# Grouped 3x3 convolution on one core: weight masks built ahead of the loads, and whole-image rows for loads and stores

## The chip, the core and the metric

The kernel runs on one core of one Trainium2 chip. The metric is the device time of one execution in microseconds (us). The core has TensorE (PE) for matmuls, VectorE (DVE), ScalarE (ACT) and GpSimd (POOL) for other work, SyncE (SP), which here only issues DMAs, and 16 DMA engines that carry every transfer. A row of a transfer is what goes to or from one of the 128 partitions of the on-chip memory; with 128 rows on 16 engines each engine has eight rows of every transfer.

## The reference

The input `x` is 16 images of 64 channels of 64x64 float32, the weight is 128 x 8 x 3 x 3. Channels are in 8 groups: 8 input channels of a group feed 16 output channels of the same group. The output is 16 x 128 x 64 x 64 float32, 33.5 MB; the input is 16.8 MB.

```python
for g in range(groups):
    for b in range(batch):
        for co in range(c_out_per_group):
            for ci in range(c_in_per_group):
                for kh in range(k):
                    for kw in range(k):
                        output[b, g * c_out_per_group + co] += \
                            weight[g * c_out_per_group + co, ci, kh, kw] * \
                            x_pad[b, g * c_in_per_group + ci, kh:kh+h, kw:kw+w]
```

## The kernel before

**Loads.** The whole input is kept on chip as bf16, in eight tiles of 128 partitions by 64x64: `xn[0..3]` holds two images each (channels on partitions), and `xs[0..3]` holds the second eight images shifted by 32 channels, so that 32-channel quarters of four images can be fed to TensorE together. The DMA converts float32 to bf16, and all loads are issued by POOL in `load` (L53). For the first group of images there are nine loads in three cuts of the image's rows (0 to 16, 16 to 32, 32 to 64), then two halves each for the other tiles: 21 loads in all. A half-image row is 8 KB of float32 in memory and 4 KB of bf16 on chip. POOL issues eight loads at once; from the ninth on, each waits until the load eight places ahead of it has landed.

**Weights.** One small load on SP's queue brings the weight. A block mask and an identity are made from memsets on DVE (L74, L84) and three `affine_select` on POOL (L75, L79, L85), which stand in the program behind the 21 loads. DVE multiplies weight and mask into `E` (L94, five instructions), TensorE transposes `E` by the identity (L107, 18 matmuls), DVE and ACT copy the results to `wN` and `wS` (L115, L117).

**Convolution.** Four groups of images, `i` = 0 to 3, four images each. A group has eight chunks of eight image rows (`c`), a chunk has nine taps by eight streams: 72 small matmuls (32 x 64 of the array each, up to 512 columns, L131), 576 in a group and 2304 in all, each with a weight load of its own. They accumulate in four PSUM banks, one per image; there are eight banks. ACT and DVE copy the four banks (L161, L163) into output tiles `ob` of 128 x 2048 float32, half an image; there are 16 such buffers. After chunks 3 and 7 of a group SP issues four stores (L168), one per image, of 1 MB each: 128 rows of 8 KB. So output leaves in eight bursts of four stores, 32 stores in all.

The program is unrolled: nothing loops on the chip, and each engine's instructions are one long list. Instructions of one engine run in program order. The order on POOL is that of the program text, which is why the masks come behind the loads there.

Of the kernel before, what the change touches and what calls it, by code (L numbers as in the profile page):

```python
# [7 lines left out]
FP32 = mybir.dt.float32  # L8
BF16 = mybir.dt.bfloat16
ALU = mybir.AluOpType  # L10


@with_exitstack
def kernel(
    ctx: ExitStack,
    tc: tile.TileContext,
    x: bass.AP,
    weight: bass.AP,
    groups: int,
    out: bass.AP,  # L20
):
    nc = tc.nc

    B, C, H, W = x.shape
    CO, CIg, K, _ = weight.shape
    G = groups
    COg = CO // G
    HW = H * W
    T = K * K
    assert (B, C, CO, K, G, H, W) == (16, 64, 128, 3, 8, 64, 64)  # L30

    R = 8
    NCH = H // R
    HALF = HW // 2

    wpool = ctx.enter_context(tc.tile_pool(name="wpool", bufs=1))
    xpool = ctx.enter_context(tc.tile_pool(name="xpool", bufs=1))
    opool = ctx.enter_context(tc.tile_pool(name="opool", bufs=16))
    psum = ctx.enter_context(tc.tile_pool(name="psum", bufs=8, space=bass.MemoryType.PSUM))

    xr = x.rearrange("b c h w -> (b c) (h w)")
    xn = [xpool.tile([128, H, W], BF16, name=f"xn{i}") for i in range(4)]
    xs = [xpool.tile([128, H, W], BF16, name=f"xs{i}") for i in range(4)]

    def flat(t):
        return t.rearrange("p h w -> p (h w)")  # L50

    def load(t, row0, p0, p1, h0, h1):
        nc.gpsimd.dma_start(  # L53
            flat(t)[p0:p1, h0 * W : h1 * W],
            xr[row0 + p0 : row0 + p1, h0 * W : h1 * W],
        )

    w_sb = wpool.tile([128, CIg * T], FP32)
    nc.sync.dma_start(w_sb, weight.rearrange("co ci kh kw -> co (ci kh kw)"))

    cuts = [0, 16, 32, 64]
    for h0, h1 in zip(cuts, cuts[1:]):
        load(xn[0], 0, 0, 128, h0, h1)
        load(xs[3], 512 - 96, 96, 128, h0, h1)
        load(xs[0], 544, 0, 128, h0, h1)
    for i in range(1, 4):
        for h0, h1 in ((0, 32), (32, 64)):
            load(xn[i], 128 * i, 0, 128, h0, h1)
            load(xs[i], 544 + 128 * i, 0, 128 if i < 3 else 96, h0, h1)

    mask = wpool.tile([128, G], FP32)
    nc.vector.memset(mask, 1.0)  # L74
    nc.gpsimd.affine_select(  # L75
        out=mask, in_=mask, compare_op=ALU.is_ge, fill=0.0,
        base=0, channel_multiplier=1, pattern=[[-COg, G]],
    )
    nc.gpsimd.affine_select(  # L79
        out=mask, in_=mask, compare_op=ALU.is_ge, fill=0.0,  # L80
        base=COg - 1, channel_multiplier=-1, pattern=[[COg, G]],
    )
    ident = wpool.tile([128, 128], BF16)
    nc.vector.memset(ident, 0.0)  # L84
    nc.gpsimd.affine_select(  # L85
        out=ident, in_=ident, compare_op=ALU.not_equal, fill=1.0,
        base=0, channel_multiplier=1, pattern=[[-1, 128]],
    )
    E = wpool.tile([128, T, 160], BF16)
    wv = w_sb.rearrange("co (ci t) -> co t ci", t=T)  # L90
    ge = 160 // CIg
    for r in range(5):
        g0 = 4 * (r % 2)
        nc.vector.tensor_mul(  # L94
            E[:, :, 32 * r : 32 * r + 32].rearrange("p t (g c) -> p t g c", c=CIg),
            wv.unsqueeze(2).to_broadcast([128, T, 4, CIg]),
            mask[:, g0 : g0 + 4].unsqueeze(1).unsqueeze(3).to_broadcast([128, T, 4, CIg]),
        )

    wN = wpool.tile([128, T, 128], BF16)  # L100
    wS = wpool.tile([128, T, 128], BF16)
    for k, (wt, off) in enumerate(((wN, 0), (wS, 32))):
        for t0 in range(0, T, 4):
            n = min(4, T - t0)
            ps = psum.tile([128, 512], FP32, name="ps", tag="ps")
            for t in range(n):
                nc.tensor.matmul(  # L107
                    ps[:, 128 * t : 128 * t + 128],
                    E[:, t0 + t, off : off + 128],
                    ident,  # L110
                    start=True, stop=True,
                )
            dst = wt[:, t0 : t0 + n, :].rearrange("p t c -> p (t c)")
            if k == 0:
                nc.vector.tensor_copy(dst, ps[:, 0 : 128 * n])  # L115
            else:
                nc.scalar.copy(dst, ps[:, 0 : 128 * n])  # L117


    outf = out.rearrange("b co h w -> b co (h w)")  # L120
    taps = [(1, 1)] + [(a, b) for a in range(3) for b in range(3) if (a, b) != (1, 1)]

    def mm(dst, wt, xt, q, half, c, kh, kw, first, last):

        lo, hi = max(0, R * c + kh - 1), min(H, R * c + R + kh - 1)
        o0 = lo - (R * c + kh - 1)
        w0, w1 = max(0, kw - 1), min(W, W + kw - 1)
        v0 = w0 - (kw - 1)
        nr, nw = hi - lo, w1 - w0
        d3 = dst.rearrange("p (h w) -> p h w", w=W)  # L130
        nc.tensor.matmul(  # L131
            d3[64 * half : 64 * half + 64, o0 : o0 + nr, v0 : v0 + nw],
            wt[32 * q : 32 * q + 32, 3 * kh + kw, 64 * half : 64 * half + 64],
            xt[32 * q : 32 * q + 32, lo:hi, w0:w1],
            start=first, stop=last,
            tile_position=(32 * q, 64 * half),
        )

    nev = 0
    for i in range(4):  # L140
        imgs = [2 * i, 2 * i + 1, 8 + 2 * i, 9 + 2 * i]
        prev = xs[i - 1]

        streams = [
            (0, wN, xn[i], 0, 0), (2, wS, xs[i], 0, 1),
            (0, wN, xn[i], 1, 1), (3, wS, xs[i], 1, 0),
            (1, wN, xn[i], 2, 0), (3, wS, xs[i], 2, 1),
            (1, wN, xn[i], 3, 1), (2, wS, prev, 3, 0),
        ]
        obs = None  # L150
        for c in range(NCH):
            if c % 4 == 0:
                obs = [opool.tile([128, HALF], FP32, name=f"ob{i}_{c}_{b}", tag="ob") for b in range(4)]
            pcs = [psum.tile([128, 512], FP32, name="ps", tag="ps") for b in range(4)]
            for k, (kh, kw) in enumerate(taps):
                for b, wt, xt, q, half in streams:
                    mm(pcs[b], wt, xt, q, half, c, kh, kw, k == 0, k == T - 1)
            for b in range(4):
                dst = obs[b][:, 512 * (c % 4) : 512 * (c % 4) + 512]
                if nev % 2 == 0:  # L160
                    nc.scalar.copy(dst, pcs[b])  # L161
                else:
                    nc.vector.tensor_copy(dst, pcs[b])  # L163
                nev += 1
            if c % 4 == 3:
                s0 = HALF * (c // 4)
                for b in range(4):
                    nc.sync.dma_start(outf[imgs[b]][:, s0 : s0 + HALF], obs[b])  # L168


# [33 lines left out]
```

## Time and profile before

| what | value |
|---|---|
| median of three runs | 147.95 us (146.76 to 151.19) |
| the profiled execution's own time | 146.28 us |
| its span, first to last instruction | 144.5 us |
| TensorE matmuls busy | 77.0 us, 2322 instructions |
| mean granted TensorE clock | 0.908 |
| moved by DMA, as the queues count it | 42.29 MB |
| read from and written to memory | 16.81 MB and 33.55 MB |

The profile is of one execution. The span is 1.78 us shorter than that execution's time. In the page's second part the span is cut into 40 slices of 3.61 us. The GB/s row counts bytes as they arrive, and a load arrives as bf16: 213 GB/s of arriving load are 426 GB/s read from memory. In the chain of waits, "issue" is time in which an engine waited for nothing that the profile shows. Some matmul records are missing from the trace, so that a count of matmuls in a row can be a little low.

### The profile page before, as it was taken

To read this page: it belongs to the slowest core of one execution; us is meant where nothing else is said; L and a number is where in the kernel's file an instruction comes from. 1 tells how busy PE (TensorE), PEld (TensorE's weight loads), DVE (VectorE), ACT (ScalarE), POOL (GpSimd) and SP (SyncE) were. 2 spreads that over 40 slices of the span, in tenths; PEclk is the share of its full clock that TensorE was granted. 3 is DMA by queue.
4 is the path that set the end of the run, shared out by engine and by line. 5 is a ranking of instruction groups with operands and counts; after the bars stand their busy time and mean duration, and the time that the engine had idled before them with its cause. 6 is when DMAs were issued, how large, how long until landed. Compare 5 with 4: busy or idle time off the path is not lost.

```text
span 144.5 us, 4928 instructions
## 1 busy us (share of the span) xinstructions
PE 77.0 (53%) x2322; PEld 51.5 (36%) x2322; DVE 45.7 (32%) x74; ACT 37.1 (26%) x68; POOL 12.0 (8%) x28
## 2 busy tenths in 40 slices
PE   0000000049966954769792993899549499930000
PEld 0000000045733632646571672566336367620000
DVE  0000000191534526117373333355603336613000
ACT  3000000003533524214352232254503325502000
POOL 6733312300000000000000000000000000000000
PEclk9999999999999999779999699599986869999655
DMA  3999999999997996995199799749999925998991
GB/s 41 118 185 214 215 215 210 213 214 217 215 206 219 426 426 277 413 410 245 75 428 413 290 426 413 295 168 401 426 426 422 415 91 211 404 426 367 428 424 75
DMA packets 7444, 42.29 MB, mean 293 GB/s; under 512 B 992, under 2 KB 992, under 8 KB 3328
## 3 DMA queue, kind: packets, MB, share of 16 engines
q1 hardware_dynamic: 4752, 33.59, 56.0%
q0 software_dynamic: 2672, 8.39, 30.4%
q8 instruction: 18, 0.29, 0.8%
q14 instruction: 2, 0.02, 0.0%
HBM read 16.81 MB, written 33.55 MB: 348 GB/s over the span
## 4 chain that ended last, share of the span: by engine, by line
PE 53%; issue 17%; DMA 16%; DVE 2%; POOL 2%; DVEq 0%; POOLq 0%
PE ps L131 52%; DMA xs<-in_x_dram 11%; DMA xn<-in_x_dram 5%; DVE E L94 2%; PE ps L107 1%; POOL xn L53 1%; POOL xs L53 1%; DVE ob L163 0%; DVEq L199 0%; POOL ident L85 0%; POOL mask L75 0%; POOLq L199 0%; POOLq L75 0%; POOLq L185 0%
## 5 line engine op out<-in xcount | busy, mean ns | idle before, releaser
L131 PE MATMUL ps<-xs,wS 32*64 32x504 bf16 (+3 forms) x1152 | 73.7, 412 | 22.6 <-issue 22.4
L131 PE MATMUL ps<-xn,wN 32*64 32x504 bf16 (+3 forms) x1152 | 74.9, 413 | 0.0
L163 DVE COPY ob<-ps 128x512 f32<-128x512 f32 x64 | 41.2, 686 | 57.5 <-PE ps L131 57.5
L131 PEld LDWEIGHTS <-wS 32*64 32x64 bf16 x1152 | 47.3, 115 | 18.6 <-issue 3.1
L161 ACT COPY ob<-ps 128x512 f32<-128x512 f32 x64 | 34.6, 589 | 63.1 <-PE ps L131 54.3
L131 PEld LDWEIGHTS <-wN 32*64 32x64 bf16 x1152 | 40.3, 115 | 29.1 <-issue 27.8
L107 PE MATMUL ps<-ident,E 128*128 128x128 bf16 x18 | 2.1, 313 | 30.8 <-DVE E L94 30.8
L107 PEld LDWEIGHTS <-E 128*128 128x128 bf16 x18 | 1.8, 147 | 30.8 <-DVE E L94 30.8
L94 DVE TENSOR_TENSOR E<-w_sb,mask 128x288 bf16<-128x288 f32 x5 | 2.9, 643 | 27.4 <-POOL mask L79 27.4
L117 ACT CAST wS<-ps 128x512 bf16<-128x512 f32 (+1 forms) x3 | 1.2, 487 | 30.3 <-PE ps L107 30.3
L53 POOL DMA_DIRECT2D xs<-in_x_dram x12 | 6.4, 536 | 9.9 <-DMA xs<-in_x_dram 7.3
L53 POOL DMA_DIRECT2D xn<-in_x_dram x9 | 5.0, 550 | 6.0 <-DMA xn<-in_x_dram 4.6
L115 DVE CAST wN<-ps 128x512 bf16<-128x512 f32 (+1 forms) x3 | 1.5, 551 | 0.1
L117 ACT ACT_TABLE_LOAD x1 | 1.3, 1283 | 0.8 <-PEq L185 0.8
L74 DVE MEMSET mask<- 128x8 f32 x1 | 0.1, 65 | 0.9 <-PEq L185 0.9
L85 POOL TENSOR_SCALAR_AFFINE_SELECT ident<-ident 128x128 bf16<-128x128 bf16 x1 | 0.3, 298 | 0.0
L75 POOL TENSOR_SCALAR_AFFINE_SELECT mask<-mask 128x8 f32<-128x8 f32 x1 | 0.2, 204 | 0.1
L79 POOL TENSOR_SCALAR_AFFINE_SELECT mask<-mask 128x8 f32<-128x8 f32 x1 | 0.2, 191 | 0.0
L185 POOL MEMSET const-float32-0.0<- 128x1 f32 x1 | 0.1, 99 | 0.3 <-issue 0.3
L84 DVE MEMSET ident<- 128x64 uint32 x1 | 0.1, 112 | 0.0
L185 POOL MEMSET const-bfloat16-1.0<- 128x1 bf16 x1 | 0.1, 102 | 0.0
L185 POOL MEMSET const-uint8-127<- 128x1 uint8 x1 | 0.1, 102 | 0.0
(1 smaller groups left out, 0.1 us busy)
## 6 DMA issues: line engine op xcount, KB each, us to landing
out_dram<-ob SPq DMA_DIRECT2D x32, 1024.0 KB, 8.8
xn<-in_x_dram POOLq DMA_DIRECT2D x7, 512.0 KB, 17.6
xs<-in_x_dram POOLq DMA_DIRECT2D x5, 512.0 KB, 16.2
xs<-in_x_dram POOLq DMA_DIRECT2D x2, 384.0 KB, 19.4
xn<-in_x_dram POOLq DMA_DIRECT2D x2, 256.0 KB, 5.8
xs<-in_x_dram POOLq DMA_DIRECT2D x2, 256.0 KB, 6.9
xs<-in_x_dram POOLq DMA_DIRECT2D x2, 64.0 KB, 5.7
xs<-in_x_dram POOLq DMA_DIRECT2D x1, 128.0 KB, 9.5
```

What stands on the lines that cost most here:

```text
L53: nc.gpsimd.dma_start(flat(t)[p0:p1, h0 * W : h1 * W], xr[row0 + p0 : row0 + p1, h0 * W : h1 * W],)
L75: nc.gpsimd.affine_select(out=mask, in_=mask, compare_op=ALU.is_ge, fill=0.0, base=0, channel_multiplier=1, pattern=[[-COg, G]],)
L79: nc.gpsimd.affine_select(out=mask, in_=mask, compare_op=ALU.is_ge, fill=0.0, base=COg - 1, channel_multiplier=-1, pattern=[[COg, G]],)
L85: nc.gpsimd.affine_select(out=ident, in_=ident, compare_op=ALU.not_equal, fill=1.0, base=0, channel_multiplier=1, pattern=[[-1, 128]],)
L94: nc.vector.tensor_mul(E[:, :, 32 * r : 32 * r + 32].rearrange("p t (g c) -> p t g c", c=CIg), wv.unsqueeze(2).to_broadcast([128, T, 4, CIg]),
L107: nc.tensor.matmul(ps[:, 128 * t : 128 * t + 128], E[:, t0 + t, off : off + 128], ident, start=True, stop=True,)
L115: nc.vector.tensor_copy(dst, ps[:, 0 : 128 * n])
L117: nc.scalar.copy(dst, ps[:, 0 : 128 * n])
L131: nc.tensor.matmul(d3[64 * half : 64 * half + 64, o0 : o0 + nr, v0 : v0 + nw], wt[32 * q : 32 * q + 32, 3 * kh + kw, 64 * half : 64 * half ...
L161: nc.scalar.copy(dst, pcs[b])
L163: nc.vector.tensor_copy(dst, pcs[b])
L185: nc = _bacc.Bacc("TRN2", target_bir_lowering=False, num_devices=1)
```

## The change

- The two memsets and the three selects move ahead: the memsets to before all loads, the selects to directly behind the first load on POOL.
- The first group is loaded in two cuts (rows 0 to 32, 32 to 64), in the order `xn[0]`, `xs[0]`, `xs[3]` (32 partitions) for each; every other tile is one load of whole images, with rows of 16 KB in memory and 8 KB on chip. There are 12 loads instead of 21.
- Output tiles are whole images (128 x 4096 float32), in eight buffers instead of 16 halves; the bytes are the same. For groups 0, 1 and 2 there is one burst of four stores of 2 MB, in rows of 16 KB, behind chunk 7. The last group is still stored in two bursts of four stores of 1 MB.

```diff
-    opool = ctx.enter_context(tc.tile_pool(name="opool", bufs=16))
+    opool = ctx.enter_context(tc.tile_pool(name="opool", bufs=8))
...
-    cuts = [0, 16, 32, 64]
-    for h0, h1 in zip(cuts, cuts[1:]):
+    mask = wpool.tile([128, G], FP32)
+    ident = wpool.tile([128, 128], BF16)
+    nc.vector.memset(mask, 1.0)
+    nc.vector.memset(ident, 0.0)
+
+    def make_masks():
+        nc.gpsimd.affine_select(
+            out=mask, in_=mask, compare_op=ALU.is_ge, fill=0.0,
+            base=0, channel_multiplier=1, pattern=[[-COg, G]],
+        )
+        nc.gpsimd.affine_select(
+            out=mask, in_=mask, compare_op=ALU.is_ge, fill=0.0,
+            base=COg - 1, channel_multiplier=-1, pattern=[[COg, G]],
+        )
+        nc.gpsimd.affine_select(
+            out=ident, in_=ident, compare_op=ALU.not_equal, fill=1.0,
+            base=0, channel_multiplier=1, pattern=[[-1, 128]],
+        )
+
+    for h0, h1 in ((0, 32), (32, 64)):
         load(xn[0], 0, 0, 128, h0, h1)
+        if h0 == 0:
+            make_masks()
+        load(xs[0], 544, 0, 128, h0, h1)
         load(xs[3], 512 - 96, 96, 128, h0, h1)
-        load(xs[0], 544, 0, 128, h0, h1)
     for i in range(1, 4):
-        for h0, h1 in ((0, 32), (32, 64)):
-            load(xn[i], 128 * i, 0, 128, h0, h1)
-            load(xs[i], 544 + 128 * i, 0, 128 if i < 3 else 96, h0, h1)
...
+        load(xn[i], 128 * i, 0, 128, 0, H)
+        load(xs[i], 544 + 128 * i, 0, 128 if i < 3 else 96, 0, H)
...
-        obs = None
+        last = i == 3
+        obs = [opool.tile([128, HW], FP32, name=f"ob{i}_{b}", tag="ob") for b in range(4)]
         for c in range(NCH):
-            if c % 4 == 0:
-                obs = [opool.tile([128, HALF], FP32, name=f"ob{i}_{c}_{b}", tag="ob") for b in range(4)]
...
-                dst = obs[b][:, 512 * (c % 4) : 512 * (c % 4) + 512]
+                dst = obs[b][:, 512 * c : 512 * c + 512]
...
-            if c % 4 == 3:
-                s0 = HALF * (c // 4)
+            n = 4 if last else NCH
+            if c % n == n - 1:
+                s0, s1 = 512 * (c + 1 - n), 512 * (c + 1)
                 for b in range(4):
-                    nc.sync.dma_start(outf[imgs[b]][:, s0 : s0 + HALF], obs[b])
+                    nc.sync.dma_start(outf[imgs[b]][:, s0:s1], obs[b][:, s0:s1])
```

More of the change, by code (lines that the diff above doesn't have):

```diff
@@ L33 @@
     NCH = H // R
-    HALF = HW // 2
     wpool = ctx.enter_context(tc.tile_pool(name="wpool", bufs=1))
     xpool = ctx.enter_context(tc.tile_pool(name="xpool", bufs=1))
-    opool = ctx.enter_context(tc.tile_pool(name="opool", bufs=16))
+    opool = ctx.enter_context(tc.tile_pool(name="opool", bufs=8))
     psum = ctx.enter_context(tc.tile_pool(name="psum", bufs=8, space=bass.MemoryType.PSUM))
@@ L59 @@
     nc.sync.dma_start(w_sb, weight.rearrange("co ci kh kw -> co (ci kh kw)"))
-    cuts = [0, 16, 32, 64]
-    for h0, h1 in zip(cuts, cuts[1:]):
+    mask = wpool.tile([128, G], FP32)
[16 more added lines that the diff above has]
+    for h0, h1 in ((0, 32), (32, 64)):
         load(xn[0], 0, 0, 128, h0, h1)
+        if h0 == 0:
+            make_masks()
+        load(xs[0], 544, 0, 128, h0, h1)
         load(xs[3], 512 - 96, 96, 128, h0, h1)
-        load(xs[0], 544, 0, 128, h0, h1)
     for i in range(1, 4):
-        for h0, h1 in ((0, 32), (32, 64)):
-            load(xn[i], 128 * i, 0, 128, h0, h1)
-            load(xs[i], 544 + 128 * i, 0, 128 if i < 3 else 96, h0, h1)
[L73 to L88, printed above, removed]
+        load(xn[i], 128 * i, 0, 128, 0, H)
+        load(xs[i], 544 + 128 * i, 0, 128 if i < 3 else 96, 0, H)
     E = wpool.tile([128, T, 160], BF16)
```

## The prediction

> **What bounds the kernel now.** I read the page first: its busy times, its slices and its chain by engine.
>
> ```profile
> PE 77.0 (53%) x2322; PEld 51.5 (36%) x2322; DVE 45.7 (32%) x74; ACT 37.1 (26%) x68; POOL 12.0 (8%) x28
> ...
> DMA  3999999999997996995199799749999925998991
> GB/s 41 118 185 214 215 215 210 213 214 217 215 206 219 426 426 277 413 410 245 75 428 413 290 426 413 295 168 401 426 426 422 415 91 211 404 426 367 428 424 75
> ...
> q8 instruction: 18, 0.29, 0.8%
> ...
> HBM read 16.81 MB, written 33.55 MB: 348 GB/s over the span
> ...
> PE 53%; issue 17%; DMA 16%; DVE 2%; POOL 2%; DVEq 0%; POOLq 0%
> ```
>
> DMA is busy for most of the span, at one rate: loads arrive at about 213 GB/s (426 read), full slices of stores show 426. At 0.426 MB per us, 50.36 MB take 118 us; the rest of the 144.5 is the start, the end and slices in which DMA starves (19, 32). So two things alternate as the bound, DMA and what feeds the stores, which is PE. Hence the chain of waits, in order of time (start, duration, what):
>
> ```profile
> 32.87 7.82 PE ps L131 x142
> 40.69 1.22 issue
> 41.91 3.66 PE ps L131 x128
> 45.57 1.44 issue
> 47.01 3.66 PE ps L131 x128
> 50.67 1.71 issue
> 52.38 3.56 PE ps L131 x119
> 55.94 2.64 issue
> 58.58 5.29 PE ps L131 x128
> 63.87 1.18 issue
> 65.05 3.66 PE ps L131 x128
> 68.71 0.89 issue
> 69.60 7.12 PE ps L131 x256
> 76.72 2.80 issue
> 79.52 8.64 PE ps L131 x242
> 88.17 2.65 issue
> 90.82 8.68 PE ps L131 x233
> 99.50 0.15 issue
> 99.64 3.56 PE ps L131 x119
> 103.20 3.46 issue
> 106.66 5.29 PE ps L131 x128
> 111.96 2.00 issue
> 113.96 12.26 PE ps L131 x384
> 126.22 2.49 issue
> 128.71 1.64 PE ps L131 x49
> ```
>
> PE stops after every 128 matmuls or a multiple of it. 128 matmuls with their weight loads are 256 instructions. Queue q8 moved 0.29 MB of instructions in 18 packets, 16 KB each; PE has 4644 instructions, 18 times 258. So I read each stop as PE waiting for its next 16 KB of instructions, which travel through the same DMA engines as the data. I call 128 matmuls a block and the time from one block's start to the next the cadence. Two windows say when it stops (us, busy times, PEclk, DMA share, GB/s):
>
> ```profile
> 96.00:116.00 20.00, 14.40 (x440) 9.66 (x425) 7.97 (x13) 6.54 (x12) 0.00 (x0) 0.88 1.00 412
> 116.00:121.00 5.00, 5.00 (x160) 3.47 (x152) 2.35 (x4) 2.15 (x4) 0.00 (x0) 0.81 0.13 48
> ```
>
> With DMA at 1.00 PE works 14.4 of 20 us; with DMA at 0.13 it never stops. The cadences: DMA idle, 3.56 (7.12 for 256), or 4.0 where the granted clock dips (12.26 for three blocks is 4.09). Under loads, 47.01 - 41.91 = 5.10 and 52.38 - 47.01 = 5.37, mean 5.2. Under stores, 58.58 - 52.38 = 6.20, 6.47, 106.66 - 99.64 = 7.02 and 7.30; I take 6.6. A 1 MB store is 8 rows on each of 16 engines, 1.049 / 0.426 = 2.46 us; call that a share. Over 3.56 the fetch loses 1.54 to 1.81 under loads (0.6 to 0.7 share) and 2.64 to 3.74 under stores (1.1 to 1.5 shares, 9 to 12 rows). It seems to queue behind whole shares, not behind one row of 2.46 / 8 = 0.31 us.
>
> **Masks early.** This is what lets PE start:
>
> ```profile
> DVE E L94 <- POOL mask L79: 27.4, 1, 27.4
> ```
> ```profile
> 27.79 0.20 POOL mask L75
> ...
> 28.40 2.32 DVE E L94 x4
> ...
> 30.77 2.10 PE ps L107 x18
> ```
> ```profile
> w_sb<-in_weight_dram SPq DMA_DIRECT2D x1, 36.0 KB, 1.9
> ```
> ```profile
> 1.29 0.67 POOL L53 DMA_DIRECT2D xn<-in_x_dram  x1 [0.78 <-POOLq L185]
> ...
> 6.31 0.56 POOL L53 DMA_DIRECT2D xs<-in_x_dram  x1 [0.68 <-DMA xn<-in_x_dram]
> ```
>
> The three selects take 28.40 - 27.79 = 0.61 and end at about 1.96 + 0.61 = 2.6; the small weight load, on SP's queue, lands 1.9 after its issue, so by about 3. E to the first convolution matmul takes 32.87 - 28.40 = 4.5: weights stand at about 7.5. Later loads on POOL are issued 0.61 later, hidden by the first load's own share of 2.46; uncovered it would cost 0.61.
>
> Now the loads hold PE. The first three (`xn[0]`, `xs[0]`, the quarter `xs[3]`) are 2.36 MB, 5.5 us at 0.426. Transfers begin at about 2.9: slice 0 holds 41 x 3.61 = 0.15 MB arriving, 0.7 us of work before 3.61. In the profile the ninth load was let go at 6.31 by the first load landing, whose 0.52 MB would be through at 2.9 + 1.2 = 4.1; so 2 us for stragglers and landing. PE starts at 2.9 + 5.5 + 2.0 = 10.4, 22.5 earlier than 32.87. Were DMA the only other bound, the end would be 2.9 + 118 and a tail of 4.3 (below): 125, the floor.
>
> **Rows of 16 KB.** The rate of DMA itself is bounded by the store slices that are full: 401 to 428 around 426 or less. All at 428 would gain 0.5% of 118, 0.6 us; all at 401 would lose 6%, 7 us. Loads (8 KB read, 4 KB arriving) and stores (8 KB) run at the same 426 although their rows differ, so I take zero. What changes is the fetch. A share doubles to 4.92. If the fetch queues by rows or by shares, its excess doubles: under stores 3.56 + 2 x (2.64 to 3.74) = 8.8 to 11.0; if 3.56 hides part of the queue, up to 2 x 6.6 = 13.2. Under loads 6.6 to 7.2, at most 10.4. If it queues by bytes, nothing changes (6.6 and 5.2). I take doubling, 10 and 7.5, nearer to the lower ends, because a loss of 9 to 12 rows, on eight rows each, looks like shares.
>
> [...]
>
> **Whole-image stores.** Groups 0 to 2 store 8.39 MB behind chunk 7: bursts of 19.7 us instead of 9.85. SP waits for the last copy of a group, and only stores are queued behind it. Eight buffers mean group 2's copies wait for group 0's stores and group 3's for group 1's; in the sum below these are 9 us or more old by then, so free; were PE as fast as in the first rival, under 2 us.
>
> **The sum**, matmul number and time. Of the blocks, 16 lie between 41.91 and 128.71 and 49 matmuls behind, so 2304 - 2048 - 49 = 207 lie ahead: fetch boundaries at 207, 335, 463 and so on. The first 207 took 41.91 - 32.87 = 9.04, with one fetch under loads in it; plus 2.3 for the longer wait.
> - Group 0: 10.4 + 11.3 = 21.7 (207), 29.2 (335), 36.7 (463), and 113 matmuls at full rate, 3.1: done at 39.8. Loads are through at about 43.5, so DMA is busy until 41 + 2.5 + 19.7 = 63.2.
> - Group 1: 44.2 (591, fetch asked at 36.7), 54.2, 64.2 (847), then DMA idle at 4.0 a block: 68.2, 72.2 (1103), done 73.7. DMA has starved for 11 us.
> - Group 2: burst 74.9 to 94.6. 76.1 (1231, already fetched), 86.1, 96.1, 100.1 (1615), done 103.6. Starved 10 us.
> - Group 3: burst 104.8 to 124.5. 104.1 (1743), 108.1 (asked before the burst), 118.1 (1999); the half group's stores queue until 134.4; 128.1 (2127), 134.7 (8 KB rows, 6.6), done 136.2.
> - Tail: before, 144.5 - 130.35 = 14.2 from the last matmul (9.85 of stores, 4.3 for the last copy, landing and end). Span 150.4.
>
> The profiled execution of before is 1.78 longer than its span: 152.2 against its 146.28, or 4% slower. That execution is 1.1% below the median of 147.95; I do not add this, and forecast 152. With both cadences at the doubled-excess minimum (8.8, 6.6) the same steps give a span of 143 (145 us), with both doubled whole 158.7 (160 us): the forecast's own range is 145 to 160. The gain of 22.5 at the start is paid back as starved DMA: in each of three groups PE gets only two blocks through a 20 us burst and makes up the others afterwards.
>
> **Rivals.** *The fetch does not lengthen (0.22).* The wait goes by bytes or by a fixed part, cadences stay 5.2 and 6.6. For it: no data row of before is 16 KB, so nothing shows the growth. Against: loss in whole shares. Steps: group 0 done at 10.4 + 9.04 + 2 x 5.2 + 3.1 = 32.9, group 1 63.8, group 2 89.3; then DMA is continuous, 90.5 + 19.7 + 9.85 = 120, and the last burst and tail take 14.2: span 134.2, 136.0 us, 7% faster. It decides when store cadences stay under about 8.
>
> [...]
>
> *Half of the excess grows (0.18).* Part is fixed latency: 8.3 and 6.3. Group 0 done at 36.3, then 70.9, 97.7, 126.9; DMA frees at 98.9 + 19.7 + 9.85 = 128.5, plus 14.2: span 142.7, 144.5 us, 1.2% faster. For it: the excess under loads is only 0.6 share, so waits are not always whole ones.
>
> **Chances.** Doubling has 0.60. 2% is what a measurement of this kernel can tell. Doubling splits 0.38 slower, 0.19 within 2%, 0.03 faster (its low end); half growth 0.11 within, 0.07 faster; no growth 0.22 faster. So 0.32 faster, 0.30 same, 0.38 slower. The range 134 to 158 leaves out what of the no-growth case lies between the floor and 134 (0.1) and the worst of doubling (0.08).
>
> **What would show it.** Convolution starting at 10 to 11 us; stops by "issue" still every 128 matmuls but two to three times as long under bursts (6 us instead of 2.6 to 3.5); DMA slices near zero after each of the first two bursts, some 10 us each; last matmul near 136. Wrong if store cadences stay below 8, if DMA never starves (then near 135), or if PE stops elsewhere than at blocks of 128.

## The result, and the profile after

The changed kernel takes 137.73 us, the median of five runs (135.59 to 139.09), against 147.95 us before, the median of five (146.62 to 151.19). Each kernel has faster and slower executions, and the ratio of the faster ones alone (135.59 and 135.77 for the changed kernel) is 0.921, with a 95% interval of 0.911 to 0.931. It is 8% faster. The forecast was 152 and slower; the first rival, at 136.0, came closest. The profiled execution took 139.08 us with a span of 137.4.

Two rows of the page's second part, in 40 slices of 3.43 us: DMA busy tenths, and GB/s.

```profile
DMA  3999999999999999995599999206999999999991
GB/s 33 179 209 217 222 217 215 212 219 212 217 243 320 336 403 410 444 410 215 234 429 396 453 410 420 119 5 279 391 437 429 410 444 394 422 425 417 420 384 62
```

DMA starves twice, in slices 18 to 19 and 25 to 27. The windows that hold these gaps and the stretch behind them (us; busy times; PEclk, DMA share, GB/s):

```profile
64.50:67.50 3.00, 3.00 (x128) 2.07 (x112) 1.29 (x2) 1.07 (x2) 0.00 (x0) 1.00 0.23 93
89.00:95.00 6.00, 5.34 (x200) 3.90 (x207) 2.58 (x4) 2.17 (x5) 0.00 (x0) 1.00 0.22 86
97.00:119.00 22.00, 14.36 (x384) 9.16 (x384) 7.73 (x12) 6.41 (x12) 0.00 (x0) 0.84 1.00 420
```

So the gaps are there, behind the first two bursts as forecast, but about 3 and 6 us long, not 11 and 10. The chain of waits in order of time (start, duration, what) has the cadences; the convolution is line 133 now.

```profile
7.27 9.90 PE ps L133 x154
17.17 1.98 issue
19.15 5.35 PE ps L133 x128
24.50 0.85 issue
25.34 3.66 PE ps L133 x128
29.01 2.53 issue
31.54 3.56 PE ps L133 x119
35.10 2.91 issue
38.01 3.61 PE ps L133 x128
...
67.89 3.66 PE ps L133 x128
71.56 3.63 issue
75.19 4.94 PE ps L133 x111
80.12 2.63 issue
82.75 3.66 PE ps L133 x128
...
97.23 3.66 PE ps L133 x128
100.89 3.63 issue
104.52 5.35 PE ps L133 x128
109.87 1.95 issue
111.81 5.35 PE ps L133 x128
117.16 1.94 issue
119.10 1.64 PE ps L133 x49
```

PE still stops only at blocks of 128. Under loads the cadence is 6.2 (19.15, 25.34, 31.54) and 6.5; under the second burst 7.3 (67.89 to 75.19), 7.6 and 6.8, and three times 7.29 from 97.23 on. The first burst, which begins while loads are still running, has 6.7, 6.6 (two blocks in 13.22) and 6.2 (38.01 to 64.16). Forecast were 7.5 under loads and 10 under stores. A second profile of the same kernel (after_again below, an execution of 138.54 us) has 7.29, 7.57 and 6.75 in the second burst and 7.57, 7.29 and 7.02 from the third on. The last matmul ends at 120.7 and DMA still has a backlog by then (a DMA share of 0.98 and 413 GB/s from 120.74 to 134).

The prediction inferred that these stops are instruction fetches. The trace's records of single packets bear it out: queue q8 has one packet of 16 KB per block, and each stop of this chain ends 1.2 to 1.6 us after such a packet has ended. For the block that starts at 67.89, the packet runs from 72.74 to 73.70 and PE resumes at 75.19. The window of 72.70 to 73.75 holds it:

```profile
q8 instruction: 1, 0.02, 5.7%
```

With DMA full the packet itself takes 0.9 to 1.0 us every time. What changes is how long after the block's start it begins: 1.1 to 1.2 us where DMA starves, 3.7 to 4.0 under loads, 4.4 to 5.3 under the second and third bursts.

### The profile page after: what moved, and what is told of

Same layout as the page of the kernel before. It is cut to its first block, busy times and chain, and to the rows that moved or that the text cites. A ratio compares the mean times of both kernels' runs of the same rounds, so it can differ in the third digit from the quotient of the medians.

```text
span 137.4 us, 4892 instructions
## 1 busy us (share of the span) xinstructions
PE 82.1 (60%) x2322; PEld 52.5 (38%) x2322; DVE 45.8 (33%) x74; ACT 37.1 (27%) x68; POOL 7.2 (5%) x19
## 4 chain that ended last, share of the span: by engine, by line
PE 60%; issue 25%; DVE 2%; DMA 1%; DVEq 0%
PE ps L133 58%; DVE E L96 2%; PE ps L109 2%; DMA w_sb<-in_weight_dram 1%; DVE ob L164 0%; DVEq L201 0%; DVEq L96 0%
## 5 line engine op out<-in xcount | busy, mean ns | idle before, releaser
L133 PE MATMUL ps<-xs,wS 32*64 32x504 bf16 (+3 forms) x1152 | 77.2, 423 | 33.5 <-issue 33.5
L133 PE MATMUL ps<-xn,wN 32*64 32x504 bf16 (+3 forms) x1152 | 80.0, 425 | 0.0
L133 PEld LDWEIGHTS <-wS 32*64 32x64 bf16 x1152 | 48.4, 118 | 21.8 <-issue 10.0
L133 PEld LDWEIGHTS <-wN 32*64 32x64 bf16 x1152 | 40.9, 118 | 40.9 <-issue 39.9
L52 POOL DMA_DIRECT2D xs<-in_x_dram x7 | 3.7, 537 | 4.1 <-DMA xs<-in_x_dram 2.3
L52 POOL DMA_DIRECT2D xn<-in_x_dram x5 | 2.9, 575 | 1.9 <-DMA xn<-in_x_dram 1.1
```

Source lines behind the costliest of these rows:

```text
L52: nc.gpsimd.dma_start(flat(t)[p0:p1, h0 * W : h1 * W], xr[row0 + p0 : row0 + p1, h0 * W : h1 * W],)
L133: nc.tensor.matmul(d3[64 * half : 64 * half + 64, o0 : o0 + nr, v0 : v0 + nw], wt[32 * q : 32 * q + 32, 3 * kh + kw, 64 * half : 64 * half ...
```

## The experiments

**The parts of the change, done alone or undone.** Median times, each with the median of the kernel before, measured beside it on the same chip:

| run | masks | loads | stores | us | before |
|---|---|---|---|---|---|
| masks_only | early | as before | half images | 133.34 | 149.61 |
| half_loads | early | half images | whole images | 138.39 | 149.61 |
| half_stores | early | whole images | half images | 132.58 | 149.61 |
| quarter_stores | early | whole images | quarter images | 134.95 | 149.61 |
| fine_tail | early | whole images | half, last group quarter | 133.24 | 148.59 |
| rows_only | late | whole images | whole images | 146.73 | 148.05 |
| after_again | early | whole images | whole images | 138.65 | 148.05 |
| half_again | early | whole images | half images | 132.56 | 148.05 |

*masks_only*: the kernel before, with memsets and selects moved as in the change and nothing else.

```diff
     for h0, h1 in zip(cuts, cuts[1:]):
         load(xn[0], 0, 0, 128, h0, h1)
+        if h0 == 0:
+            make_masks()
```

> The kernel before with the masks moved early and nothing else: rows of 8 KB, half images, 21 loads and 32 stores stay. Theory A (the early masks bring the gain, and long rows cost a little through longer instruction fetches): PE starts at about 7 to 10 us, cadence 5.2 under loads and 6.6 under stores; 207 matmuls at 18.5, 16.4 further blocks at about 6.2, PE ends near 120, plus 14.2: span 132 to 136, as fast as the changed kernel or up to 3% faster. Theory B (the long rows bring part of the gain, by fewer DMAs and longer unbroken transfer): over 2% slower than the changed kernel, 140 us or more.

133.34 us (132.52 to 133.81): theory A's time. Its steps fit less well: PE waits for a load of `xs` until 19.25, 207 matmuls are reached at 22.95 and not at 18.5, and the cadences are 5.9 to 6.7 where DMA is full, under loads and stores alike. The masks alone give at least as much as the whole change does (135.59 to 139.09 in the five runs above, 137.99 to 139.50 in four more below). The four were on another chip, but the kernel with half-image stores, run on both, took 132.58 and 132.56. DMA starves only once, in slice 35 (115.2 to 118.5 us), as the last matmuls run:

```profile
DMA  2899999999999999999999999999999999949990
```

*half_loads*:

```diff
-        load(xn[i], 128 * i, 0, 128, 0, H)
-        load(xs[i], 544 + 128 * i, 0, 128 if i < 3 else 96, 0, H)
+        for h0, h1 in ((0, 32), (32, 64)):
+            load(xn[i], 128 * i, 0, 128, h0, h1)
+            load(xs[i], 544 + 128 * i, 0, 128 if i < 3 else 96, h0, h1)
```

> The changed kernel with the loads of groups 1 to 3 in half images again (8 KB read per row), stores as changed. Theory A: the load cadence falls from 6.2 to 5.2 for about 5 blocks, group 0 is done some 3 us earlier, DMA starves less; 132 to 136 us. Theory B: 137 us or more.

138.39 us, the time of the changed kernel. The number is theory B's, but its reason is not borne out: the load rows make no difference that can be measured. The cadence under loads was 6.20 with 8 KB rows too (blocks starting at 18.33, 24.53 and 30.73), so theory A's step from 6.2 to 5.2 was wrong.

*half_stores*, and the same kernel again (*half_again*) beside the changed one (*after_again*) on one chip:

```diff
-            n = 4 if last else NCH
+            n = 4
```

> The changed kernel with all groups stored as the last one is, in two bursts of four stores of 1 MB (8 KB rows), loads as changed. Theory A: the store cadence falls from 7.3 to about 6.6, the first burst starts half a group earlier, DMA starves at most 3 us in all; 130 to 135 us. Theory B: 138 us or more.

> The changed kernel once more, beside the half-image stores on the same chip: 135 to 139 us.

> Half-image stores with everything else of the change, beside the changed kernel on the same chip. If bursts of 2 MB stores and the starving between them are what the changed kernel loses: 132 to 133 us, 2% to 4% faster than it. If the earlier difference was the chip: within 2% of it.

132.58, and then 132.56 against 138.65 on one chip: 4.4% less. Their ratios to before are 0.902 (0.894 to 0.911) and 0.944 (0.935 to 0.953). Half-image stores beat both kernels; whole-image stores cost the change about 6 us on this chip (3 against its two quickest runs on record, 135.59 and 135.77). The chain of half_again, in a stretch with DMA full throughout:

```profile
68.46 3.66 PE ps L133 x128
72.13 2.26 issue
74.39 3.66 PE ps L133 x128
78.05 2.26 issue
80.31 5.35 PE ps L133 x128
85.65 0.57 issue
86.23 3.56 PE ps L133 x119
```

The cadence is 5.92 three times running, even where a granted clock of 0.68 stretches the matmuls of a block to 5.35.

*quarter_stores*, stores of 0.5 MB behind every second chunk, and *fine_tail*, this for the last group alone:

```diff
-            n = 4 if last else NCH
+            n = 2
```

```diff
-            n = 4 if last else NCH
+            n = 4 if i < 3 else 2
```

> The changed kernel with stores of two chunks each: bursts of four stores of 0.5 MB in rows of 4 KB, loads as changed. Theory A: shares of 1.23 us, the fetch waits less, store cadence 4.5 to 6, last burst 5 us shorter; 124 to 131 us. Theory B: rows of 4 KB cost rate and DMAs are many: 138 us or more.

> Half-image stores for groups 0 to 2 (bursts of four 1 MB stores) and two-chunk stores (0.5 MB, 4 KB rows) for the last group, whole-image loads, masks early. The half-image run starved DMA for some 4 us around the last group. If that is what still separates it from the DMA floor: 128 to 131 us, against 132.6 for half images. If small stores cost as much as in the all-quarter run: 132 to 134.

134.95 and 133.24: neither theory's numbers for quarters, and for the finer tail the second guess, no gain over half images. The chain of quarter_stores, rows of 4 KB, a share of 1.23 us:

```profile
79.47 3.66 PE ps L133 x128
83.13 2.26 issue
85.39 5.12 PE ps L133 x75
```

5.92 again: half the share, the same cadence. DMA did not starve, but from 64 to 100 us, where DMA was full in both, it ran at 414 GB/s and in half_again at 421.

*rows_only*: the selects behind the 12 loads again.

```diff
-        if h0 == 0:
-            make_masks()
...
         load(xs[i], 544 + 128 * i, 0, 128 if i < 3 else 96, 0, H)
+    make_masks()
```

> The changed kernel with the three selects behind all loads again: rows of 16 KB, whole-image stores, masks late. With 12 loads in place of 21 POOL reaches the selects earlier than before (it waits for the load eight places ahead, which are now larger: some 20 to 27 us). If the early masks bring the whole gain: PE starts 15 to 20 us later than in the changed kernel, DMA starves between the bursts, 146 to 153 us, no faster than before. If the rows bring part of it: 140 us or less.

146.73 us (143.31 to 149.42 in ten runs), not told apart from 148.05 (146.20 to 153.48 in thirteen). What let E go, by the waits:

```profile
DVE E L95 <- POOL mask L70: 13.0, 1, 13.0
```

With 12 loads POOL reaches the selects at 13 us, not at 20 to 27 as I expected, and PE starts 14 us earlier than before (18.5). Even so no clear gain is measured: the rows and whole-image bursts cost about what this earlier start is worth. How much of it is the bursts, this run alone does not tell.

**A stream beside PE.** To price the fetch by itself, these kernels convolve group 0's tiles four times over, keep the results on chip, and let SP store a constant tile; only the form of the stores differs. The edit of bg_16k_8rows, without the lines that leave out loads and results:

```diff
+    cst = opool.tile([128, HW], FP32, name="cst", bufs=1)
+    nc.vector.memset(cst, 0.5)
+    for b in range(B):
+        nc.sync.dma_start(outf[b], cst)
```

> The disputed cost by itself. The kernel loads group 0's tiles only and convolves them four times over (so all matmuls are there), its results stay on chip, and SP sends 33.5 MB of a constant tile to the output without waiting for anything: one steady stream of 79 us beside PE, then a quiet rest. Left out: the loads of groups 1 to 3 and the storing of results. Here the stream is 32 stores of 1 MB, eight rows of 8 KB on each engine. All theories: cadence as in the half-image runs under stores, 5.9 to 6.6, and 3.5 to 4.1 when the stream has ended.

> The same with 16 stores of 2 MB, eight rows of 16 KB on each engine, the form of the changed kernel. By bytes (a fetch waits for about as many bytes whatever the rows): 5.9 to 6.6. By what the changed kernel showed: 6.7 to 7.6. By whole shares or by rows, as predicted: 8.8 to 11.

> The same with 16 stores of 2 MB, but sixteen rows of 8 KB on each engine (two images, half an image each). If the length of the row sets the wait: as with 1 MB stores of 8 KB rows, 5.9 to 6.6. If the size of the DMA sets it: as with 2 MB stores of 16 KB rows, 6.7 to 7.6 or more. By bytes: 5.9 to 6.6.

> The same with 32 stores of 1 MB, four rows of 16 KB on each engine (64 partitions each). If the length of the row sets the wait: 6.7 to 7.6. If the size of the DMA sets it, or bytes: 5.9 to 6.6.

> Steady stream beside PE as before (loads of groups 1 to 3 and the storing of results left out): 16 stores of 2 MB in 16 KB rows, but from four different tiles and to the images in the order of the changed kernel. The single-tile stream had cadences of 5.9 to 6.7, mean 6.2; the changed kernel 7.3 under the same rows. If the source tiles or the images make the difference: 7.0 to 7.6. If not: 5.9 to 6.7.

The chain of bg_8k_16rows (2 MB stores, 8 KB rows), and then of bg_16k_8rows (2 MB stores, 16 KB rows), DMA share 1.0 in both:

```profile
43.81 3.66 PE ps L138 x128
47.47 2.26 issue
49.73 5.35 PE ps L138 x128
```

```profile
63.52 3.66 PE ps L134 x128
67.18 2.53 issue
69.71 5.02 PE ps L134 x110
```

The cadences are 5.92 with 8 KB rows in 2 MB stores and 6.19 with 16 KB rows. All blocks in full streams: 8 KB rows in 1 MB stores 5.92 to 6.20; 8 KB rows in 2 MB stores 5.9 to 6.2; 16 KB rows 5.92 to 6.74, mean 6.2, and from four tiles 5.9 to 6.2. Twice the share costs 0.0 to 0.3 us (0.8 in one block), not 2.6 to 3.7. That ends the doubling.

One stream does not fit: bg_16k_4rows, with 64 partitions to a store, was slower, 6.7 to 8.1. By its own condition that points at the length of the row, but the streams of 128 partitions with the same rows do not show it. Why it is slower stays open.

*bg_2k_8rows* (256 KB stores) shows that a full DMA alone does not make 5.92.

> Steady stream as in the 1 MB run, but 128 stores of 256 KB, eight rows of 2 KB on each engine, a share of 0.6 us. If the extra wait of about 2.4 us is a fixed number of bytes or a fixed latency of a busy DMA engine: 5.9 to 6.2 as with 8 KB rows, as long as DMA stays busy. If it is a number of rows or shares: 4.2 or less. If the issuing queue cannot keep DMA busy with such small stores, cadence falls and the DMA share shows it.

Two windows of this run (us; busy times; PEclk, DMA share, GB/s):

```profile
18.00:24.00 6.00, 3.66 (x128) 2.45 (x128) 2.58 (x4) 2.15 (x4) 0.00 (x0) 1.00 1.06 402
24.00:38.00 14.00, 11.25 (x400) 7.90 (x407) 6.45 (x10) 5.96 (x11) 0.00 (x0) 1.00 1.05 399
```

The block from 18.29 to 24.21 took 5.92, the next three 4.56, 4.27 and 4.55, with DMA full in both windows. After 40 us, with DMA no longer full (348 GB/s to 80 us, against 426 with 16 KB rows), they take 4.0 to 4.6. So the wait can be shorter with DMA full. Whether the short rows, the small stores or the number of stores that wait in the queue do it is not told apart (SP waited 97 times for an earlier store to land).

**Bursts.** Constant tiles again, but each group's stores are let go by its last copy.

```diff
+        nc.vector.tensor_copy(cs[i][:, 0:1], dst[:, 0:1])
+        for b in (2 * i, 2 * i + 1, 8 + 2 * i, 9 + 2 * i):
+            nc.sync.dma_start(outf[b], cs[i])
```

> The same 16 stores in four bursts of four, each let go by the last copy of a group, as in the changed kernel (constant tiles are stored, loads of groups 1 to 3 left out). If the burst makes the difference (a queue that is filled once and runs out, with DMA idle ahead of it): 6.7 to 7.6 inside bursts. If not: 5.9 to 6.7. In both, 3.5 to 4.1 between the bursts.

> The burst run again (constant tiles let go by the last copy of a group, loads of groups 1 to 3 and storing of results left out), each burst of the same 8.4 MB as eight stores of 1 MB in rows of 8 KB. With 16 KB rows cadences inside bursts were 6.8 to 7.3, mean 7.1. If bursts alone make it: the same 7.1. If row length matters in a burst: 5.9 to 6.6.

> The burst run with 8 KB rows once more, now with both halves of each constant tile let go by the last copy of a group (before, the stores of the second halves had nothing to wait for and ran ahead as a steady stream). Four bursts of eight 1 MB stores; loads of groups 1 to 3 and the storing of results left out. With 16 KB rows cadences inside bursts were 6.8 to 7.3. If bursts alone make it: 6.8 to 7.3. If row length matters in a burst: 5.9 to 6.6.

In bg_8k_burst the stores of the second halves ran ahead as a stream (5.9 to 6.2, and 5.9 to 6.5 in the bursts of four that were left), so it did not test what it was meant to. The chains of bg_16k_burst and of bg_8k_burst_b, where both halves wait:

```profile
63.34 3.66 PE ps L135 x128
67.01 3.63 issue
70.64 5.35 PE ps L135 x128
```

```profile
65.74 3.66 PE ps L135 x128
69.40 3.63 issue
73.03 4.87 PE ps L135 x112
```

7.30 with 16 KB rows and 7.29 with 8 KB rows; all blocks inside bursts take 6.7 to 7.3 in both. The 7.3 of the changed kernel comes with stores let go in bursts of 8.4 MB, whatever their rows. An idle DMA ahead of the burst is not enough: in bg_8k_burst a burst of four 1 MB stores on an idle DMA had a block of 5.92 (89.74 to 95.66). By the packet records a fetch begins 4.4 to 5.1 us after its block's start inside these bursts of 8.4 MB, and 3.5 to 3.9 us after it in the streams of 8 KB rows; the packet takes 0.9 to 1.0 us in both. Why it waits longer in a burst was not settled.

## Why the prediction was wrong

**Masks early: right, with a term mis-sized.** PE's first convolution matmul came at 7.27, not 10.4. Weights stood when forecast (7.5), and E then waited for the weight's load, no longer for the mask:

```profile
DVE E L96 <- DMA w_sb<-in_weight_dram: 1.8, 1, 1.8
```

The first matmuls run on the first load; the first one that reads `xs` starts at 10.00, near the 10.4 that I forecast for having the first three loads. 207 matmuls were reached at 19.15, against 21.7: from 10.00 they took 9.15, about the 9.04 of before, so the 2.3 that I added for a longer fetch did not come.

**Rows of 16 KB: the step that failed.** It read: "A share doubles to 4.92. If the fetch queues by rows or by shares, its excess doubles", and took 10 and 7.5. Under stores the changed kernel shows 6.2 to 7.6, and the streams, where only the form of the stores changes, show 5.92 for shares of 2.46 us and for 2 MB stores of short rows (4.92), and 6.2 for 16 KB rows; quarter_stores has 5.92 for a share of 1.23. The excess of before, 1.1 to 1.5 shares, looked like a count of shares, but I had one size of store only, and one size cannot show a proportion. A wait that does not grow with the store fits it as well, and that was the first rival.

**Cadence under loads: mis-read.** My 5.2 came from the two blocks after 41.91. Windows of before (us; busy times; PEclk, DMA share, GB/s):

```profile
41.91:47.01 5.10, 3.67 (x129) 2.44 (x128) 2.58 (x4) 2.15 (x4) 0.00 (x0) 1.00 0.81 218
47.01:52.38 5.37, 3.66 (x128) 2.43 (x128) 2.58 (x4) 2.15 (x4) 0.00 (x0) 1.00 1.02 423
```

In the first the loads were ending and DMA was not full; the second ran under stores alone (423 GB/s). Neither is a cadence under full loads. With DMA full of loads it is mostly 6.2 (5.9 to 6.5 in the changed kernel and half_loads), whether rows are 8 or 16 KB.

**DMA's own rate: right.** Streams of 16 KB rows moved 426 GB/s and of 8 KB rows 422; the zero I took for it stands.

**Whole-image stores: the term that was missing.** I gave them nothing but idle time. They also make bursts of 8.4 MB, in which the cadence is about 7.3 and not 5.9. My 6.6 was a mean over before's half-size bursts, 6.2 to 7.3.

**The sum holds with the measured cadences.** They come from the execution that is being explained, so this tests the steps and not the prices. The same steps with 6.2 and 7.3, from 19.15: group 0 done at 34.7; DMA busy until 63; group 1 66.3; burst 67.5 to 87.2; group 2 93; burst and half group 94.3 to 123.9; last matmul 121; the last burst and tail of 14.2 from 123.9 give 138.1. Measured: group 1 at 65.5, group 2 at 92.6, the last matmul at 120.7, the span 137.4. So blocks, boundaries, bursts and tail were right, and the sign turned mainly on one price, that of a fetch.

**The rivals.** The first had the mechanism (no growth with the row) and nearly the time. Its span of 134.2 is 3.2 short of the profiled 137.4, since its cadences (5.2 and 6.6) were both too low; it left out the bursts. That 137.73 lies within my range of 134 to 158 is due to this rival, which the range took in, and not to the step that I forecast from. The half-growth rival (144.5) has no support: there is next to no growth to halve.

**Stops where DMA starves and where it is full.** In the changed kernel PE stopped for 0.22 us at 67.67, where DMA starves (a share of 0.23 from 64.50 to 67.50), and for 2.5 to 3.6 us where DMA is full (shares of 1.01 to 1.06 in these stops), behind blocks that ran at the full clock (1.00).

## What to carry to other kernels

This unrolled PE program fetched its instructions by DMA while its data moved (18 packets of 16 KB on queue q8), and PE stopped at its blocks of 128 matmuls. In another kernel look whether PE stops at equal counts of matmuls, and price the stop with DMA starving, full and in bursts (here 0.22 us at 67.67 of the changed kernel, 2.26 in half_again and 3.63 in bg_16k_burst). When a wait is to be scaled to a new size, first ask whether the profile has it at two sizes; one size shows a duration, not a law. Where DMA and its producer share the bound, send output early and often enough that DMA never starves (here half-image stores took 132.56 us against 138.65); a larger transfer brought nothing here, since the rate was full already (426 against 422 GB/s).

## What the runs showed that I had not expected

- With DMA full, a block of 128 matmuls took 5.92 us in run after run, with store rows of 4 or 8 KB and stores of 0.5, 1 or 2 MB; the cadences differ by steps of about 0.27 (5.92, 6.20, 6.47, 6.74, 7.02, 7.29).
- The packet of a fetch takes 0.9 to 1.0 us with DMA full; what grows is the time before it begins, from 1.1 us after the block's start where DMA starves to 3.5 to 3.9 in a stream of 8 KB rows and up to 5.3 in a burst.
- Stores in bursts of 8.4 MB make the block 6.7 to 7.6, also with the same rows as in a stream.
- At 5.92 a block a lower clock cost nothing in half_again: with a granted clock of 0.68 the matmuls of a block took 5.35 us (3.66 at 1.00) and still fit, with 0.57 to spare.
